# Gate and up projections of 18 feed-forward tiles as seven block products over 2x2x2 blocks

## The chip, the cores and the metric

The kernel runs on one core of a Trainium2 chip. The metric is the device time of one execution in microseconds (us). The core has five engines that run side by side: TensorE (PE) multiplies matrices, VectorE (DVE) and ScalarE (ACT) work element by element, GpSimd (POOL) and SyncE (SP) issue DMAs. Each takes its instructions in the order in which the program issued them. PEld in the profile is TensorE's loading of weights, which overlaps its matmuls.

## The reference

Two layers of a backbone over 512 latent tokens and 256 context tokens, 1024 wide: a modulated RMS norm, attention beside a long convolution, a gated merge, an output projection, and then a feed-forward part. The part that the change touches is the feed-forward:

```python
def swiglu(h, w_gate_up, w_down):
    g, u = jnp.split(h @ w_gate_up, 2, axis=-1)
    return (jax.nn.silu(g) * u) @ w_down

for layer in range(DEPTH):          # DEPTH = 2
    ...
    if not last:
        ctx = ctx + c_gate2 * swiglu(modulate(rms_norm(ctx, ...), c_shift2, c_scale2), ...)
    x = x + gate2 * swiglu(modulate(rms_norm(x, ...), shift2, scale2), ...)
```

The inner width is 2816, that is 22 tiles of 128. Layer one (index 0) runs it over all 768 tokens, layer two over the 512 latent ones.

## The kernel before

Everything is kept transposed: a tile holds 128 channels in the partitions and the tokens along the free axis. Each float32 operand is split into a high part and a low part of a shorter format (`fp32r`), and a product is the sum of three matmuls, high by high, high by low and low by high (`mm3`, L237). For weights the split is one ACT copy (`act`, L248) and one DVE subtraction (`tt`, L258). Weights come by DMA into one of five `raw` buffers; `w_load` (L333) splits each into a `hi` and a `lo` buffer (four of each, 1024 columns wide), and `w_more` (L353) starts the next load when a `raw` is free, in the order of a list, `plan` (L311).

The order of the work is made while the kernel is built. Each piece of work is a Python generator that yields what it needs: tiles, free buffers, events. `Order.go` (L159) keeps an estimate of each engine's time from fixed costs. Among the tasks that are ready by TensorE's time it takes the one of lowest priority number, else the one that is ready first, and so writes one fixed instruction order for each engine. Buffers are counted too: 37 of `s` (768 wide), 13 of `f` (1024 wide), eight PSUM banks `ps`; `t` is a short-lived `s`.

The feed-forward of a layer (L1385) goes by groups of tiles, `GROUPS`, six, six, six and four. For each tile `job` (L548) streams all eight k blocks of the gate weights, first over tokens 0 to 512, then 512 to 768, 24 matmuls each; then the same for up. The first two tiles of a layer use `pair_job` (L575), gate and up side by side. `g_evac` makes tanh on ACT and a product on DVE (`stt`, L254); `u_evac` multiplies by up and splits the result into a pair `pr`, which goes into `mids`. When a group's tiles are through, the down projection multiplies its `mids` for eight output tiles, and `resid` (L1216) adds each to the stream `xs` on DVE. The first two output tiles run as a `pair_job`, k block by k block, so that the last of `mids` is needed last. The last group runs through `parts` (L595) over the token ranges `END` (0 to 256, 256 to 512, 512 to 768), so that the next layer's norm can begin.

Beside this runs `mod_rest` (L444): the rest of the modulation vectors, 80 tiles of 128 channels, each a 512 KB DMA into a `raw` buffer and one or two multiply-and-reduce instructions on DVE (L458). It is spawned once in layer one at `j == START` (L1306) and again ahead of the merge (L1360), with priority 0; tiles from `CALM` on, and those of layer two, wait until the norms before the feed-forward are done.

## Time and profile before

| what | value |
|---|---|
| median of 3 runs | 2166.92 us (2166.75 to 2167.97) |
| the profiled execution: its time | 2169.32 us |
| its span, first to last instruction | 2167.5 us |
| mean granted TensorE clock | 0.994 of full speed |
| moved by DMA | 256.72 MB, mean 118 GB/s |
| longest stretch of the last chain on TensorE alone | 521.48 us from 753.29 us, in layer one's feed-forward |

The span runs from the first to the last instruction; the device time also has what lies around it. A stage's rows give busy time by engine. In a group of instructions, "busy" is the sum over the group, "mean ns" the duration of one, and "idle before" the time its engine stood still just ahead of them, with what ended most of it. Matmuls overlap, so what one costs is read from the distance between their starts.

### The profile page before, as it was taken

What the parts mean: (1) busy time and instruction counts of PE and PEld (TensorE: products, weight loads), DVE (VectorE), ACT (ScalarE), POOL (GpSimd) and SP (SyncE); (2) the same over time, 40 slices, a digit from 0 to 9 for tenths busy, and PEclk for the clock granted to TensorE, in tenths of its full rate; (3) what the DMA queues carried; (4) which work ended last, traced back from release to release, by engine and by line L of the source; (5) the groups of instructions that cost most, each with busy time, mean ns of one, the idle gap of its engine ahead of it and who ended that gap; (6) DMA issues with size and microseconds to landing.
All of it is one profiled execution on the core that took longest, in us unless ns stands there. A gap on an engine that the chain in (4) does not pass through costs nothing.

```text
span 2167.5 us, 30309 instructions
## 1 busy us (share of the span) xinstructions
PE 2129.8 (98%) x12001; PEld 1837.0 (85%) x12001; DVE 1388.0 (64%) x2550; ACT 732.1 (34%) x1336; POOL 117.1 (5%) x218
## 2 busy tenths in 40 slices
PE   8999999999999999999999999999999999999997
PEld 2889888888888888888888897887888898888887
DVE  5878637767896798743333468756877665434354
ACT  3433223445522421131221334223545343222231
POOL 2112100001000000000000010200001000000000
PEclk9999999999999999999999999999999999999999
DMA  9234422113375267832212332532213433323231
GB/s 361 74 125 160 144 73 73 40 60 126 108 232 186 79 200 227 266 99 73 66 52 78 107 109 85 190 100 89 73 54 117 154 133 96 109 81 110 80 110 39
DMA packets 83053, 256.72 MB, mean 118 GB/s; under 512 B 10668, under 2 KB 15183, under 8 KB 82912
## 3 DMA queue, kind: packets, MB, share of 16 engines
q1 hardware_dynamic: 63840, 197.43, 27.9%
q0 software_dynamic: 19072, 57.36, 8.2%
q8 instruction: 94, 1.54, 0.3%
q14 instruction: 47, 0.39, 0.1%
HBM read 232.07 MB, written 22.68 MB: 118 GB/s over the span
## 4 chain that ended last, share of the span: by engine, by line
PE 88%; DVE 7%; issue 3%; ACT 1%; DMA 1%; POOL 0%; SPq 0%; DVEq 0%; ACTq 0%; POOLq 0%
PE ps L234 85%; PE ps L244 3%; DVE f L258 2%; DVE s L254 2%; DVE s L258 1%; DVE lo L258 1%; ACT s L248 1%; DVE mx L269 0%; DMA s<-in_rcos 0%; DVE ss L269 0%; DVE s L263 0%; DVE rq L258 0%; DMA f<-in_wmodf 0%; ACT hi L248 0%; DVE rq L254 0%
## 5 line engine op out<-in xcount | busy, mean ns | idle before, releaser
L234 PE MATMUL ps<-s,hi 128*128 128x512 f32 (+1 forms) x4288 | 1132.5, 353 | 8.9 <-ACT s L248 5.9
L234 PEld LDWEIGHTS ps<-s,hi 128*128 128x128 f32 x4288 | 749.1, 190 | 117.8 <-ACT s L248 8.7
L234 PE MATMUL ps<-s,lo 128*128 128x512 f32 (+1 forms) x2144 | 751.0, 350 | 0.1
L234 PEld LDWEIGHTS ps<-s,lo 128*128 128x128 f32 x2144 | 406.4, 190 | 54.3 <-DVE lo L258 0.6
L248 ACT ACTIVATE hi<-raw 128x1024 fp32r<-128x1024 f32 (+2 forms) x272 | 268.6, 995 | 469.0 <-PE ps L234 329.9
L258 DVE TENSOR_TENSOR lo<-raw,hi 128x1024 fp32r<-128x1024 f32 (+2 forms) x272 | 309.1, 1142 | 100.0 <-ACT hi L248 97.6
L234 PE MATMUL ps<-f,hi 128*128 128x512 f32 (+1 forms) x1184 | 297.0, 341 | 0.0
L254 DVE SCALAR_TENSOR_TENSOR s<-s,ps 128x512 f32<-128x512 f32 (+1 forms) x184 | 107.0, 586 | 267.6 <-ACT s L248 143.7
L234 PEld LDWEIGHTS ps<-f,hi 128*128 128x128 f32 x1184 | 205.0, 190 | 25.3
L248 ACT ACTIVATE s<-ps 128x256 f32<-128x256 f32 (+5 forms) x234 | 107.7, 482 | 314.9 <-PE ps L234 236.4
L234 PE MATMUL ps<-f,lo 128*128 128x512 f32 (+1 forms) x592 | 201.5, 340 | 0.0
L254 DVE SCALAR_TENSOR_TENSOR s<-ps,mod,s 128x256 f32<-128x256 f32 (+1 forms) x144 | 82.9, 585 | 152.0 <-PE ps L234 151.7
L234 PE MATMUL ps<-hi,s 128*128 128x512 f32 x512 | 165.2, 395 | 0.0
L234 PE MATMUL ps<-f 128*128 128x256 f32 (+1 forms) x1014 | 141.9, 289 | 4.0 <-DMA f<-in_fw 3.8
L248 ACT ACTIVATE f<-ps 128x512 fp32r<-128x512 f32 (+3 forms) x184 | 91.3, 538 | 137.4 <-PE ps L234 85.5
L234 PEld LDWEIGHTS ps<-f 128*128 128x128 f32 (+1 forms) x1014 | 129.5, 191 | 7.3 <-DMA f<-in_z 3.8
L234 PEld LDWEIGHTS ps<-f,lo 128*128 128x128 f32 x592 | 112.2, 189 | 12.6
L248 ACT ACTIVATE s<-ps,nb 128x256 f32<-128x256 f32 (+1 forms) x144 | 80.7, 568 | 109.0 <-DVE nb L263 105.0
L234 PEld LDWEIGHTS ps<-hi,s 128*128 128x128 f32 x512 | 97.0, 189 | 19.5
L458 DVE CUSTOM_DVE_ANT_0 raw<-raw,f 128x1024 f32<-128x1024 f32 x80 | 97.9, 1224 | 23.7 <-DMA raw<-in_wmodt 21.9
L269 DVE TENSOR_REDUCE mx<-ps 128x1 f32<-128x512 f32 (+1 forms) x104 | 68.4, 684 | 61.0 <-PE ps L234 61.0
L258 DVE TENSOR_TENSOR f<-ps,f 128x512 fp32r<-128x512 f32 (+2 forms) x144 | 90.7, 654 | 24.9 <-ACT f L248 24.1
(118 smaller groups left out, 1803.8 us busy)
## 6 DMA issues: line engine op xcount, KB each, us to landing
raw<-in_w_gu SPq DMA_DIRECT2D x88, 512.0 KB, 3.7
raw<-in_wmodt SPq DMA_DIRECT2D x80, 512.0 KB, 4.3
raw<-in_w_down SPq DMA_DIRECT2D x48, 384.0 KB, 3.2
raw<-in_w_gate SPq DMA_DIRECT2D x32, 512.0 KB, 3.7
raw<-in_w_hy SPq DMA_DIRECT2D x24, 512.0 KB, 4.6
raw<-in_w_qkv SPq DMA_DIRECT2D x24, 512.0 KB, 3.7
raw<-in_w_out SPq DMA_DIRECT2D x24, 512.0 KB, 3.9
f<-in_tab POOLq DMA_DIRECT2D x40, 256.0 KB, 5.2
```

Source lines behind the costliest of these rows:

```text
L234: nc.tensor.matmul(out=o, lhsT=l, rhs=r, start=start, stop=stop)
L244: nc.tensor.transpose(o, x, ident[0:n, 0:n])
L248: nc.scalar.activation(out=o, in_=i, func=f, **kw)
L254: nc.vector.scalar_tensor_tensor(out=o, in0=a, scalar=s, in1=b, op0=op0, op1=op1)
L258: nc.vector.tensor_tensor(out=o, in0=a, in1=b, op=op)
L269: nc.vector.tensor_reduce(out=o, in_=a, op=op, axis=AX.X)
L458: nc.vector.tensor_tensor_reduce(out=junk[:, 0:D], in0=raw, in1=cond[s], scale=1.0, scalar=0.0, op0=ALU.mult, op1=ALU.add, accum_out=mraw[ ...
```

## The change

Gate and up of tiles 4 to 21 in layer one are computed together. With the weights cut into two halves of k (four blocks of 128 each) by gate and up, and the activations into the two halves of k by two halves of the tokens (384 each), the result is a 2x2 block product. It is made from seven block products in place of eight (Strassen's scheme in Winograd's form). Each product streams 4 k blocks x 3 matmuls of 384 columns.

- `s_load` gets the two raw weight tiles of a feed-forward tile, makes four sums of weight halves on DVE and splits the seven forms, each 512 columns, into halves of the `hi` and `lo` buffers.
- `s_forms` makes four forms of the activations once, for all 18 tiles. From the second k block on, and for the form T3, which is written over part of the activations themselves, it waits until the first group's plain products are issued (`plain`).
- `s_job` issues the seven products; `sums` adds them up on DVE into gate and up (`g`, `c`), `silu` and `times` do by halves of the tokens what `g_evac` and `u_evac` did.
- Groups in layer one: 4, 4, 4, 2, 4 and 4 tiles; the first of these is computed as before. Layer two keeps its groups.
- `w_load` takes its buffers in the order of the list (`turn`), and the last group's down weights wait for `room`.
- `mod_rest` runs at priority 0 or 3 and fetches one tile ahead. `START` 5 is beyond the loop over j, so only the second call does work. Some priorities, the number of attention lanes, the order of gate jobs and how far loads run ahead have other values.

```diff
-GROUPS = ((0, 6), (6, 6), (12, 6), (18, 4))
+GROUPS = (((0, 4), (4, 4), (8, 4), (12, 2), (14, 4), (18, 4)), ((0, 6), (6, 6), (12, 6), (18, 4)))
+PLAIN = (4, 22)
+LATE = 1
+MODP = (0, 3)
+FORMP = (0, 0, 1)
+HALF = TOK // 2
...
-LANES, MORE_LANES = (2, 10), (4, 5)
+LANES, MORE_LANES = (2, 9), (1, 4)
-CALM = 40
+CALM = 43
-START = 3
+START = 5
-FIRST_W, AHEAD = 4, 2
-CONV, SPEC, TURN, ROPE, LANE, HYP, NORM2, LONG, STORE, SPLIT = -3, 3, 4, -1, 4, -10, 4, 3, 4, -5
+FIRST_W, AHEAD = 4, 3
+CONV, SPEC, TURN, ROPE, LANE, HYP, NORM2, LONG, STORE, SPLIT = -3, -2, 4, -5, 4, -12, 2, 3, 3, -5
-MIX = ((4, 2, 2, 1), (3, 2, 2, 1))
+MIX = ((4, 2, 2, 1), (4, 2, 4, 1))
...
     def w_load(i, src, nk, nf, one=False):
...
-        yield [raw_n] + ([("f", 1)] if one else [("hi", 1), ("lo", 1)])
-        if one:
+        room = Cond(lambda: len(od.free["f"]) > 3 or gu_done[0].set and (od.free["f"] or len(od.free["s"]) > 20))
+        yield [raw_n, turn[i]] + ([room] if one else [("hi", 1), ("lo", 1)])
+        if one and not od.free["f"]:
+            tiles = [new("t", F32R) for _ in range(2)]
+            hi, lo = tiles[0][:, 0:n], tiles[1][:, 0:n]
+        elif one:
...
+    def s_load(i, src):
+        g, u = new("raw"), new("raw")
+        for x, y in zip((g, u), (src[0], src[1])):
+            dma(x.rearrange("p (k f) -> p k f", k=KD), y, nc.sync)
+        halves = lambda x: (x[:, 0:512], x[:, 512:1024])
+        (g0, g1), (u0, u1) = halves(g), halves(u)
...
+        steps = ((g0, ()), (g0, ((u0, u0, u1, ALU.add), (g0, u0, g0, ALU.subtract))), (g1, ()),
+                 (g0, ((g1, g1, g0, ALU.subtract), (g0, u1, g0, ALU.subtract))), (u0, ()), (g1, ()), (u1, ()))
+        for e, (x, ops) in zip(res, steps):
+            for o, y, z, op in ops:
+                yield [y, z]
+                tt(o, y, z, op)
+            f = yield from forms.place()
...
+            hi, lo = [y.rearrange("p k f -> p (k f)") for y in f[0]]
+            yield [x]
+            act(hi, x)
+            yield [hi]
+            tt(lo, x, hi, ALU.subtract)
...
+    def prod(form, b):
+
+        yield [form, ("ps", 1)]
+        o = new("ps")[:, 0:HALF]
+        (wh, wl), tiles, left = form.form
+        for k in range(4):
+            yield [b[k][2]]
+            yield [wh[:, k, :], wl[:, k, :], b[k][0], b[k][1]]
+            mm3(o, wh[:, k, :], wl[:, k, :], b[k][0], b[k][1], k == 0, k == 3)
+        forms.done(tiles, left)
+        return o
+
+    def s_job(B, pr, got):
...
+        def times(sl, o):
+            yield [cut[sl is b], got]
+            yield [o]
+            stt(t[:, sl], t[:, sl], 0.5, o, ALU.mult, ALU.mult)
+            yield [t[:, sl]]
+            act(pr[0][:, sl], t[:, sl])
+            yield [pr[0][:, sl]]
+            tt(pr[1][:, sl], t[:, sl], pr[0][:, sl], ALU.subtract)
...
+        def sums():
...
+            act(g[:, a], P[0])
...
+            tt(g[:, b], g[:, a], P[1], ALU.add)
...
+            tt(g[:, a], g[:, a], P[2], ALU.add)
...
+            tt(c[:, a], g[:, b], P[3], ALU.add)
...
+            tt(g[:, b], g[:, b], P[4], ALU.add)
+            tt(c[:, b], c[:, a], P[4], ALU.add)
...
+            tt(g[:, b], g[:, b], P[5], ALU.add)
...
+            tt(c[:, a], c[:, a], P[6], ALU.add)
...
+        for n, (x, y) in enumerate(((A11, B11), (S2, T2), (A12, B21), (S3, T3), (S1, T1), (S4, B22), (A22, T4))):
+            P[n] = yield from prod(x, y)
+            made[n].set = True
+
+    def s_forms(h, B, plain):
...
+            if k == LATE:
+                yield [plain]
...
+            tt(a, ah, al, ALU.add)
+            tt(b, bh, bl, ALU.add)
+            tt(a[:, a_], a[:, b_], a[:, a_], ALU.subtract)
+            tt(a[:, b_], b[:, b_], a[:, b_], ALU.subtract)
+            tt(b[:, b_], b[:, b_], a[:, a_], ALU.subtract)
+            tt(b[:, a_], b[:, a_], b[:, b_], ALU.subtract)
...
-                    od.spawn(mod_rest(stop, [stop]), 0)
+                    od.spawn(mod_rest(stop, [stop]), MODP[0])
...
-                od.spawn(mod_rest(Event(), calm), 0)
+                od.spawn(mod_rest(Event(), calm), MODP[1])
...
-            for gi, (f0, fn) in enumerate(GROUPS):
+            plain = Event()
+            if not last:
...
+                od.spawn(s_forms(h, B, plain), FORMP[0])
+            for gi, (f0, fn) in enumerate(GROUPS[l]):
                 mids = []
                 for f in range(f0, f0 + fn):
...
+                    if f >= PLAIN[l]:
+                        pr, got = [], Event()
+                        if f < FFT - 1:
+                            yield [("f", 2)]
+                            pr += [new("f", F32R) for _ in range(2)]
+                            got.set = True
+                        yield from s_job(B[0:7], pr, got)
+                        mids.append(pr)
+                        if f == FFT - 1:
+                            drop(*[x for p in h for x in p], *B[7])
+                            yield [("s", 2)]
+                            pr += [new("s", F32R) for _ in range(2)]
+                            got.set = gu_done[l].set = True
+                        continue
```

More of the change, by code (lines that the diff above doesn't have):

```diff
@@ L344, in w_load @@
             hi, lo = tiles[0][:, 0:n], tiles[1][:, 0:n]
-        loaded[i] = [x.rearrange("p (k f) -> p k f", k=nk) for x in (hi, lo)] + [tiles]
+        turn[i + 1].set = True
+        loaded[i] = [x.rearrange("p (k f) -> p k f", k=nk) for x in (hi, lo)] + [tiles, one]
         w_here[i].set = True
@@ L351, in w_load, with __init__, place, done @@
         w_more()
+    class Forms:
+        def __init__(self):
+            self.half = None
+        def place(self):
+            if self.half:
+                tiles, left = self.half
+                self.half = None
+                c = 512
+            else:
+                yield [("hi", 1), ("lo", 1)]
+                tiles, left = [new("hi", F32R), new("lo", F32R)], [2]
+                self.half = tiles, left
+                c = 0
+            return [x[:, c:c + 512].rearrange("p (k f) -> p k f", k=4) for x in tiles], tiles, left
+        def done(self, tiles, left):
+            left[0] -= 1
+            if not left[0]:
+                drop(*tiles)
+                at[2] -= 1
+                w_more()
@@ new lines, in hyena_body @@
+    forms = Forms()
+    def s_load(i, src):
[4 more added lines that the diff above has]
+        (g0, g1), (u0, u1) = halves(g), halves(u)
+        res = loaded[i] = [Event() for _ in range(7)]
+        for e in res:
+            e.form = None
+        w_here[i].set = True
+        yield [g, turn[i]]
+        steps = ((g0, ()), (g0, ((u0, u0, u1, ALU.add), (g0, u0, g0, ALU.subtract))), (g1, ()),
[5 more added lines that the diff above has]
+            f = yield from forms.place()
+            e.form, e.set = f, True
+            if e is res[-1]:
+                turn[i + 1].set = True
+            hi, lo = [y.rearrange("p k f -> p (k f)") for y in f[0]]
[3 more added lines that the diff above has]
+            tt(lo, x, hi, ALU.subtract)
+        drop(g, u)
+        w_more()
@@ L353, in w_more @@
     def w_more(upto=INF):
         while at[1] < min(len(plan), upto) and od.free["raw"]:
-            one = len(plan[at[1]]) > 3
-            if not od.free["f"] if one else at[2] >= SLOTS["hi"] + AHEAD:
+            e = plan[at[1]]
+            if len(e) == 1:
+                if len(od.free["raw"]) < 2:
+                    break
+                at[1] += 1
+                at[2] += 4 - at[3] % 2
+                at[3] += 1
+                od.spawn(s_load(at[1] - 1, *e), FORMP[2])
+                continue
@@ L357, in w_more @@
+            one = len(e) > 3
+            if not (od.free["f"] or len(od.free["s"]) > 8) if one else at[2] >= SLOTS["hi"] + AHEAD:
                 break
@@ L446, in mod_rest, with fetch @@
         yield from load_cond(cond)
-        while rest and not stop.set:
-            yield [("raw", 1)]
-            if rest[0][1] >= CALM or rest[0][0]:
-                yield calm
-                yield [("raw", 1)]
+        ahead = []
+        early = lambda: rest[0][1] < CALM and not rest[0][0] or all(e.set for e in calm)
+        def fetch():
             l, t, both = rest.pop(0)
@@ L454, in mod_rest @@
             dma(raw, I["wmodt"][l, t], nc.sync)
+            ahead.append((l, t, both, raw))
+        while ahead or rest and not stop.set:
+            if not ahead:
+                yield [("raw", 1)]
+                if not early():
+                    yield calm
+                    yield [("raw", 1)]
+                fetch()
+            if rest and not stop.set and len(od.free["raw"]) > 1 and early():
+                fetch()
+            l, t, both, raw = ahead.pop(0)
             yield [raw, ("t", 1), "DVE"] + cond
@@ new lines, in s_forms, with third @@
+    def s_forms(h, B, plain):
+        a_, b_ = slice(0, HALF), slice(HALF, TOK)
+        B11, B21, B22, T1, T2, T3, T4 = B[0:7]
+        for k in range(4):
+            (ah, al), (bh, bl) = h[k], h[k + 4]
+            if k == LATE:
+                yield [plain]
+            yield [ah, al, bh, bl, ("f", 2), ("t", 4 if k % 2 == 0 else 2)]
+            a, b = new("f"), new("f")
+            a, b = a[:, 0:TOK], b[:, 0:TOK]
+            tA = [new("t", F32R) for _ in range(2)]
+            if k % 2 == 0:
+                tB = [new("t", F32R) for _ in range(2)]
+                B[7].extend(tB)
+            B[7].extend(tA)
+            tt(a, ah, al, ALU.add)
[4 more added lines that the diff above has]
+            tt(b[:, a_], b[:, a_], b[:, b_], ALU.subtract)
+            h2 = b_ if k % 2 else a_
+            for form, x, sl in ((T1, tA, a_), (T2, tA, b_), (T4, tB, h2)):
+                form[k][0:2] = [y[:, sl] for y in x]
+                form[k][2].set = True
+            for x, (hi, lo, _) in ((b[:, b_], T2[k]), (a[:, a_], T1[k]), (b[:, a_], T4[k])):
+                yield [x]
+                act(hi, x)
+                yield [hi]
+                tt(lo, x, hi, ALU.subtract)
+            drop(b)
+            def third(a=a, k=k):
+                yield [plain]
+                act(T3[k][0], a[:, b_])
+                yield [T3[k][0]]
+                tt(T3[k][1], a[:, b_], T3[k][0], ALU.subtract)
+                drop(a)
+                T3[k][2].set = True
+            od.spawn(third(), FORMP[1])
@@ L1426, in program @@
                     mids.append(pr)
+                    plain.set = f == PLAIN[l] - 1
                 yield [x[:, 40:48] for x in m[0:2 - last]]
-                if gi == len(GROUPS) - 1:
-                    drop(*[x for p in h for x in p])
+                if gi == len(GROUPS[l]) - 1:
+                    if last:
+                        drop(*[x for p in h for x in p])
                     end = stag if last else END
```

87 lines of the change are left out of this document (76 added, 11 removed).

## The prediction

> **What bounds the kernel now.** I read the page first: who is busy, and the chain that ended last.
>
> ```profile
> span 2167.5 us, 30309 instructions
> PE 2129.8 (98%) x12001; PEld 1837.0 (85%) x12001; DVE 1388.0 (64%) x2550; ACT 732.1 (34%) x1336; POOL 117.1 (5%) x218
> PE 88%; DVE 7%; issue 3%; ACT 1%; DMA 1%; POOL 0%; SPq 0%; DVEq 0%; ACTq 0%; POOLq 0%
> ```
>
> TensorE is busy for 98% of the span, and 88% of the last chain is its own instructions. A busy PE need not be an efficient one, so the next question is where it is ever idle. The windows view answers by stage (columns: window, its length, then busy us with the number of instructions of PE, PEld, DVE, ACT, POOL, then clock, DMA share, GB/s):
>
> ```profile
> 0.00:55.00 55.00, 45.56 (x125) 13.27 (x126) 32.26 (x70) 21.27 (x36) 11.71 (x26) 0.94 0.99 356
> 520.00:604.00 84.00, 81.83 (x545) 73.04 (x544) 75.96 (x169) 43.47 (x111) 6.79 (x12) 1.00 0.42 141
> 604.00:690.00 86.00, 86.00 (x479) 75.32 (x478) 77.21 (x120) 21.19 (x25) 2.15 (x4) 1.00 0.67 223
> 690.00:753.00 63.00, 62.56 (x380) 55.33 (x379) 40.93 (x83) 23.21 (x37) 0.00 (x0) 1.00 0.25 83
> 753.00:1275.00 522.00, 521.99 (x3058) 464.14 (x3057) 284.44 (x463) 116.55 (x178) 0.00 (x0) 1.00 0.39 123
> 1275.00:1310.00 35.00, 30.34 (x203) 26.71 (x203) 31.97 (x96) 18.12 (x42) 10.76 (x20) 0.99 0.46 144
> 1475.00:1700.00 225.00, 220.74 (x1266) 192.01 (x1266) 170.90 (x356) 114.12 (x263) 17.17 (x32) 1.00 0.29 93
> ```
>
> The feed-forward of layer one fills 753 to 1275 us (its first tiles begin a little before). PE is idle there for 0.01 us of 522, at full clock: this stage costs exactly the columns that it streams. DVE has 284 of 522 busy, ACT 117. So fewer streamed columns shorten it one for one, as long as nobody else becomes late.
>
> **What the products save.** What a matmul costs is its spacing, not its duration, which overlaps the next. The timeline of PE alone (start, us, operation) shows one gate or up job, eight k blocks of three matmuls, first over 512 tokens, then over 256:
>
> ```profile
> 823.78 0.63 PE L234 MATMUL ps<-s,hi 128*128 128x512 f32 x2
> 829.25 0.40 PE L234 MATMUL ps<-s,hi 128*128 128x256 f32 x2
> 832.12 0.63 PE L234 MATMUL ps<-s,hi 128*128 128x512 f32 x2
> 840.46 0.63 PE L234 MATMUL ps<-f,hi 128*128 128x512 f32 x2
> ```
>
> 24 matmuls of 512 take 829.25 - 823.78 = 5.47 us, 0.228 each; 24 of 256 take 2.87, 0.1196 each. Gate and up of one tile: 840.46 - 823.78 = 16.68 us. No row has 384 columns; the bounds are 0.1196 (a 256) and 0.228 (a 512). I take the middle, 0.1738, since the two points give a line of 0.42 ns a column with 11 ns on top, and loading weights keeps pace even with 256-column matmuls. A new tile is seven products of 4 x 3 matmuls of 384: 84 x 0.1738 = 14.60 us, **2.08 less**, and 18 tiles give **37.4 us**. At the ends of the bound a tile is 10.0 or 19.2, the second slower than now; a cost that jumps between 256 and 512 is excluded by nothing but the line, and it goes to the slow rival. The Trainium skill, "TensorE: Matmul & The Clock Gate", section Back-to-back issue gap, gives N/2.4 + 2.5 ns for an isolated matmul; by it a tile would go from 15.6 to 13.65 us and the saving would be an estimated 35 us. The trace's 0.228 and 0.1196 lie 10 ns above the page's 0.216 and 0.109, so the rows decide.
>
> The down projection keeps its columns: six groups instead of four split the same 22 tiles.
>
> **What it adds on DVE and ACT.** The groups by line in the same stage (count | busy us, mean ns | idle before):
>
> ```profile
> L458 DVE CUSTOM_DVE_ANT_0 raw<-raw,f 128x1024 f32<-128x1024 f32 x56 | 68.5, 1223 | 22.9 <-DMA raw<-in_wmodt 21.9
> L258 DVE TENSOR_TENSOR lo<-raw,hi 128x1024 fp32r<-128x1024 f32 x44 | 53.7, 1222 | 14.7 <-ACT hi L248 14.7
> L254 DVE SCALAR_TENSOR_TENSOR s<-s,ps 128x512 f32<-128x512 f32 x44 | 30.1, 685 | 83.5 <-ACT s L248 46.2 <-PE ps L234 37.1
> L458 DVE CUSTOM_DVE_ANT_0 s<-raw,f 128x1024 bf16<-128x1024 f32 x24 | 29.2, 1217 | 0.4 <-DMA raw<-in_wmodt 0.4
> L258 DVE TENSOR_TENSOR lo<-raw,hi 128x768 fp32r<-128x768 f32 x24 | 22.7, 955 | 4.0 <-ACT hi L248 4.0
> L254 DVE SCALAR_TENSOR_TENSOR s<-s,ps 128x256 f32<-128x256 f32 x44 | 18.4, 418 | 34.9 <-ACT s L248 23.8 <-PE ps L234 10.8
> L254 DVE SCALAR_TENSOR_TENSOR s<-ps,mod,s 128x512 f32<-128x512 f32 x24 | 17.8, 749 | 35.4 <-PE ps L234 35.4
> L254 DVE SCALAR_TENSOR_TENSOR s<-ps,mod,s 128x256 f32<-128x256 f32 x35 | 16.4, 481 | 27.9 <-PE ps L234 27.9
> L258 DVE TENSOR_TENSOR f<-s,f 128x512 fp32r<-128x512 f32 x17 | 11.7, 690 | 8.4 <-ACT f L248 8.4
> L258 DVE TENSOR_TENSOR f<-s,f 128x256 fp32r<-128x256 f32 x17 | 7.1, 417 | 0.0
> L458 DVE DVE_READ_ACCUMULATOR2_ANT mraw<- 128x1 f32 x80 | 6.5, 82 | 0.0
> L258 DVE TENSOR_TENSOR f<-raw,f 128x512 fp32r<-128x512 f32 x8 | 5.3, 686 | 1.3 <-ACT f L248 1.3
> L248 ACT ACTIVATE f<-s 128x512 fp32r<-128x512 f32 x17 | 10.8, 633 | 96.2 <-DVE s L254 96.2
> L248 ACT ACTIVATE f<-s 128x256 fp32r<-128x256 f32 x17 | 6.9, 408 | 8.2 <-DVE s L254 7.9
> ```
>
> A tile now costs DVE 2 x 1.222 (weights) + 2 x (0.685 + 0.418) (tanh product, times up) + 0.690 + 0.417 (low part) = 5.76 us. After: weights, 4 sums and 7 low parts of 512, 11 x 0.686; evacuation, 7 sums, 2 + 2 products and 2 low parts of 384, 13 x 0.553 (midway between 0.417 and 0.690, the ends of the bound). 7.55 + 7.19 = **14.74 us**, against 14.60 on PE. That looks like a tie, but these durations overlap a little: the twelve DVE rows above add up to 287, without the smaller groups, where the window has 284 busy. I allow up to 8% off: 13.6 to 14.7.
>
> DVE recovers in the down pass. Four tiles of down are 8 x 4 x 3 matmuls of each size, 96 x (0.228 + 0.1196) = 33.4 us of PE, and on DVE 8 x (0.686 + 0.749 + 0.481) = 15.3. So a group of four has 4 x 14.60 + 33.4 = 91.8 us on PE and 4 x 14.74 + 15.3 = 74.3 on DVE, 81%. Forms can be split ahead into eight half buffers (four hi and lo pairs), more than one tile's seven, so DVE has about a tile's slack inside a group. ACT: 7 splits at 0.633 and 5 pieces at about 0.52 (midway of 0.408 and 0.633), 7.0 us a tile: never the bound.
>
> Once per layer: the activation forms, per k block 2 x 0.955 + 8 x 0.553, four times 25.3 us, written while the plain first group (4 x 16.68 + 33.4 = 100 us of PE) runs. The two extra groups add 16 x (0.749 + 0.481) = 19.7 us. In all DVE gains 18 x 9.0 + 25.3 + 19.7 = about 207 us on top of 284, in a stage of 485: **near full**. What decides is whether full DVE means late PE. These stretches of before say no:
>
> ```profile
> 756.00:790.00 34.00, 34.00 (x200) 30.18 (x199) 33.24 (x56) 9.45 (x15) 0.00 (x0) 1.00 0.56 184
> 790.00:835.00 45.00, 45.00 (x258) 39.71 (x258) 44.13 (x76) 11.15 (x18) 0.00 (x0) 1.00 0.65 203
> 1000.00:1100.00 100.00, 100.00 (x585) 88.77 (x584) 34.97 (x48) 20.67 (x29) 0.00 (x0) 1.00 0.22 70
> ```
>
> From 756 to 835 DVE has 77.4 of 79 busy, and PE loses nothing; later DVE is at 35%. The filler is the modulation reduction (the two custom groups, 97.7 us). After, it runs at priority 3, below the form and evacuation tasks at 0, so it yields: with 36 us free in the plain group (100 - 4 x 5.76 - 15.3 - 25.3) and 17 to 25 in each later one, it ends between 1030 and 1190 us instead of 925, and only the next layer wants it.
>
> **What it adds as waits.** Down cannot start before the last tile's `mids` are there. Each hop has a price: a job's last matmul of three starts at 707.62, the next job 0.23 later, and DVE answers at 708.05.
>
> ```profile
> 707.62 0.39 PE L234 MATMUL ps<-s,lo 128*128 128x512 f32 x1
> 708.05 0.75 DVE L254 SCALAR_TENSOR_TENSOR s<-ps,mod,s 128x512 f32<-128x512 f32 x1 [3.30 <-PE ps L234]
> ```
>
> After the seventh product: 0.20 + three DVE steps of 0.553 + one ACT step of 0.52 = 2.4 us alone; the other half's chain (begun one product, 2.09 us, earlier) and one or two weight splits of 0.686 stand in the same queue: 3.2 to 3.9. The cover is the down job's first blocks: 3 x 6 x 0.228 = 4.1 us with four tiles, so nothing to 1 us more when a reduction of 1.22 cuts in (three ends, I take 0.5 each); 6 x 0.228 = 1.37 in the group of two: 2.0; 18 x 0.1196 = 2.15 before the last block in the last group, which starts on 256 tokens: 1.5. Sum **5.0 us** (bounds 0 and 19: at worst each of five ends waits 3.9 less the smallest cover, plus a reduction). Behind these waits only the down matmuls are queued. In the last group at most one down weight is split ahead; the second costs 0.633 + 0.686 = 1.3 us in the shadow of the same chain.
>
> **What moves elsewhere.** Four early reduction tiles (from 204 to 251 us) go away from there, with two broadcasts on POOL's queue, and `CALM` 43 lets three more run early.
>
> ```profile
> L277 SPq DMA_DIRECT2D raw<-in_wmodt x80: 327/328/1554, 182.5 to 919.3; - x80
> L458 DVE CUSTOM_DVE_ANT_0 s<-raw,f x4: 1215/1215/1217, 203.8 to 249.6; 128x1024 bf16<-128x1024 f32 x4
> L458 DVE CUSTOM_DVE_ANT_0 raw<-raw,f x16: 1224/1224/1228, 604.2 to 668.9; 128x1024 f32<-128x1024 f32 x16
> raw<-in_w_gu SPq DMA_DIRECT2D x88, 512.0 KB, 3.7
> ```
>
> So 7 x 2.44 = 17 us more of DVE between 540 and the norm near 716; before, the last ends at 670, so it ends near 690, in the 690 to 753 stage with 22 us free. On SP's queue there are 16 more issues of 0.33 us, hidden like its others; a new tile's two raw blocks land 3.7 us after issue, two of the five raw buffers hold a pair, and the next pair has 14.6 us to come. Other lanes, gate order and priorities: the stages around hold 2.2 + 0.4 + 4.7 + 4.3 = 11.6 us of PE idle in the windows above that they could win or about double. I take 0, bounds -8 and +10.
>
> **Sum.** -37.4 + 5.0 + 0 = -32.4. The profiled execution took 2169.3 us (span 2167.5 and 1.8 around it); it goes to 2136.9. It lay 2.4 above the median 2166.9, so the median goes to **2134.5 us**.
>
> **Rivals.**
> - *DVE partly late.* If each tile runs at DVE's 14.74 plus 0.7 of waits that its queue can't fill, 0.84 x 18 = 15 us are lost: 2150. For: 81% in a group, full with the reductions. Against: 756 to 835. It includes ends that stall over 3.4 us; there the Trainium skill (same page, section on the clock gate) has a rule that an idle window of about 3.4 us halves the clock. In this trace the 0 to 55 stage with 9.4 us idle had 0.94, the one at 1275 with 4.7 us in pieces 0.99, so it adds little. 0.17.
> - *DVE in strict order behind ACT: slower.* Each of the nine low parts needs the ACT result just before it, and two products need a tanh. If the queue can't fill these eleven waits, DVE needs 14.74 + 7 x 0.633 + 4 x 0.52 = 21.3 us a tile. Break-even is 16.68, with 1.94 of those 6.5 exposed; at half (18.0) the tiles lose 61 us and the kernel goes to 2195. The Trainium skill, "VectorE: DVE Perf Modes", section on the TRN2 errata, speaks against small pieces too: a fixed cost per instruction, so at least 512 elements. The rows agree (1.222 at 1024, 0.417 at 256: 0.15 us fixed), and it is in the sum. Against the rival: 14.7 us idle behind ACT in 44 low parts now. With matmuls of 384 costing over 0.1986 (16.68/84), the other way to lose, 0.06.
> - *The retuning wins as well*: 8 us of the idle elsewhere, 2126. 0.12.
> - *No gain reaches the end*: the layer boundary after 1275 waits for the late reductions or DMAs instead. It would need 32 us; the reductions have 50 us of margin, and the first sixteen, which the next norm reads, far more. 0.03.
>
> **Chances.** The forecast has 0.62 (2128 to 2144). A measurement tells 0.2%, 4 us, from no change. Faster: 0.62 + 0.12 + 0.16 of the partly late case = 0.90; same 0.04 (0.01 of that case and the last); slower 0.06. The range takes in the retuning's gain and most of the partly late case: 2120 to 2156, with 0.83 inside.
>
> **What would show it.** Right: in the feed-forward of layer one 1512 matmuls of 384 columns spaced 0.174 us, a stage shorter by 30 to 37 us, DVE 85% or more busy, reductions on beyond 1000 us. Wrong: PE waits for `hi` or `lo` inside a tile (DVE is the bound), waits over 2 us at the ends of groups of four, spacing over 0.18, or stages outside that differ by over 10 us.

## The result and the profile after

The changed kernel takes **2153.02 us**, the median of four runs (2148.8 to 2155.55), against 2167.14 for the kernel before beside it (2166.75 to 2167.97): a ratio of **0.9932, 95% interval 0.9915 to 0.9950**. It is 14 us faster where 32 were forecast. (Of the kernels below, two had one run far longer than the rest at a lower granted clock, as had the kernel before; medians and ratios leave these out.) The profiled execution took 2152.17 us, 17.15 less than that of before.

The first lines of the page after:

```profile
span 2150.4 us, 30465 instructions
PE 2100.6 (98%) x11785; PEld 1839.0 (86%) x11785; DVE 1567.1 (73%) x2926; ACT 786.8 (37%) x1476; POOL 115.1 (5%) x216
PE 69%; DVE 18%; issue 5%; DMA 5%; ACT 1%; SPq 0%; POOL 0%; DVEq 0%; ACTq 0%; POOLq 0%
```

TensorE's busy time fell by 29.2 us (2129.8 to 2100.6), the span by only 17.1. And the last chain has changed hands: DVE holds 18% of it instead of 7, DMA 5 instead of 1. TensorE's timeline inside the products (start, us, operation):

```profile
862.07 0.51 PE L246 MATMUL ps<-s,hi 128*128 128x384 f32 x2
...
881.83 0.51 PE L246 MATMUL ps<-s,hi 128*128 128x384 f32 x2
```

From 862.07 to 881.83 lie 38 sets of three, 114 matmuls in 19.76 us: 0.1733 each, without a gap. The saving is there. The windows view of after shows where it went (busy us of PE, PEld, DVE, ACT, POOL; then clock, DMA share, GB/s):

```profile
690.00:750.00 60.00, 56.88 (x334) 51.01 (x332) 52.60 (x93) 21.41 (x32) 0.00 (x0) 0.94 0.45 142
750.00:800.00 50.00, 49.69 (x285) 43.43 (x285) 44.23 (x89) 16.11 (x29) 0.00 (x0) 1.00 0.37 113
800.00:900.00 100.00, 97.60 (x557) 91.62 (x557) 94.95 (x172) 34.49 (x67) 0.00 (x0) 0.98 0.30 95
900.00:1000.00 100.00, 97.66 (x553) 92.80 (x552) 93.18 (x168) 32.14 (x60) 0.00 (x0) 0.98 0.42 133
1000.00:1100.00 100.00, 96.13 (x548) 88.84 (x547) 88.19 (x161) 28.51 (x54) 0.00 (x0) 1.00 0.48 157
1100.00:1200.00 100.00, 99.75 (x573) 95.18 (x573) 89.42 (x161) 35.20 (x65) 0.00 (x0) 1.00 0.41 130
1200.00:1262.00 62.00, 59.41 (x391) 58.97 (x390) 51.66 (x103) 27.34 (x51) 0.00 (x0) 1.00 0.34 107
1262.00:1300.00 38.00, 36.13 (x223) 31.09 (x223) 32.78 (x99) 18.63 (x42) 10.75 (x20) 1.00 0.45 132
```

A stage loses PE's idle time, plus its length times what the clock falls short of 1. The feed-forward lost 0.01 us before (753 to 1275); now its six rows, 750 to 1262, have 11.8 us idle, and two have clock 0.98, 2 us each: about 16. The stage ahead of it (690 to 750) has 3.1 idle and clock 0.94, 6.7 together, against 0.4 before. DVE has 462 of 512 us busy in the feed-forward, up to 95% in a stretch.

To close the account over the whole trace, I added up how far each matmul stands from the next beyond the usual distance of its shape (0.227, 0.173 and 0.120 us for 512, 384 and 256 columns). That loss was 56.4 us before and is 77.4 after. With the feed-forward taken from 744 to 1275 us before and from 750 to 1262 after, it went there from 2.5 to 20.7; in the stretch from 604 us up to it from 0.5 to 6.6; everywhere else from 53.4 to 50.1, with gains and losses. Saved columns: 18 x (48 x (0.227 + 0.120) - 84 x 0.173) = 38.2 us. 38.2 less 21.0 is 17.2, the 17.1 of the spans.

The two largest waits of TensorE between 760 and 1262 us (us in total, times, longest):

```profile
PE ps L246 <- ACT f L260: 5.7, 4, 2.3
PE ps L246 <- DVE f L270: 3.0, 3, 2.0
```

What DVE did around the stall at 912 us, and then TensorE, by the timeline:

```profile
908.73 1.23 DVE L556 CUSTOM_DVE_ANT_0 s<-raw,f 128x1024 bf16<-128x1024 f32 x1
...
910.00 1.23 DVE L556 CUSTOM_DVE_ANT_0 raw<-raw,f 128x1024 f32<-128x1024 f32 x1
...
911.15 1.01 DVE L270 TENSOR_TENSOR f<-f,ps 128x384 f32<-128x384 f32 x2
912.08 0.68 DVE L270 TENSOR_TENSOR lo<-raw,hi 128x512 fp32r<-128x512 f32 x1
912.68 1.61 DVE L266 SCALAR_TENSOR_TENSOR f<-f 128x384 f32<-128x384 f32 x3
```

```profile
908.17 0.33 PE L246 MATMUL ps<-s,lo 128*128 128x384 f32 x1
...
912.24 0.39 PE L246 MATMUL ps<-f,lo 128*128 128x512 f32 x1
914.91 1.39 PE L246 MATMUL ps<-f,hi 128*128 128x512 f32 x2 [2.28 <-ACT f L260]
```

The group's last product ends near 908.4. Its last sums start on DVE only at 911.15, behind a pair of reductions that began at 908.73. PE covers 4 us with the first blocks of down and then stands still for 2.28 us. No line names the reduction as the culprit: the waits view names the last hop, ACT. One has to read DVE's queue backwards from there. The other large stalls up to here: 3.0 us at 714.8 (the out-projection's sum behind reductions up to 713.84), 2.0 at 820.4, 1.5 at 1008.3, 1.75 at 1070.2 and 2.0 at 1241.5. All of PE's waits in the feed-forward from 760 us on stand at ends of groups, none inside a tile.

### The profile page after: what moved, and what is told of

Its sections match the earlier page's. It is cut to its first block, busy times and chain, and to the rows that moved or that the text cites. A ratio compares the mean times of both kernels' runs of the same rounds, so it can differ in the third digit from the quotient of the medians.

```text
span 2150.4 us, 30465 instructions
## 1 busy us (share of the span) xinstructions
PE 2100.6 (98%) x11785; PEld 1839.0 (86%) x11785; DVE 1567.1 (73%) x2926; ACT 786.8 (37%) x1476; POOL 115.1 (5%) x216
## 4 chain that ended last, share of the span: by engine, by line
PE 69%; DVE 18%; issue 5%; DMA 5%; ACT 1%; SPq 0%; POOL 0%; DVEq 0%; ACTq 0%; POOLq 0%
PE ps L246 67%; DVE lo L270 3%; DVE f L270 3%; DMA raw<-in_wmodt 3%; PE ps L256 2%; DVE s L266 2%; DVE raw L556 2%; DVE s L556 2%; DMA f<-in_wmodf 1%; DVE f L266 1%; DVE s L270 1%; DVE raw L270 1%; ACT s L260 1%; DVE mx L281 1%; DMA f<-in_tab 0%
## 5 line engine op out<-in xcount | busy, mean ns | idle before, releaser
L246 PE MATMUL ps<-s,hi 128*128 128x512 f32 (+2 forms) x4112 | 1097.4, 352 | 7.0 <-ACT s L260 3.1
L246 PEld LDWEIGHTS ps<-s,hi 128*128 128x128 f32 x4112 | 728.3, 189 | 91.4 <-ACT s L260 5.4
L246 PE MATMUL ps<-s,lo 128*128 128x512 f32 (+2 forms) x2056 | 719.9, 350 | 0.1
L260 ACT ACTIVATE hi<-raw 128x512 fp32r<-128x512 f32 (+3 forms) x378 | 307.3, 832 | 491.5 <-PE ps L246 301.6
L270 DVE TENSOR_TENSOR lo<-raw,hi 128x512 fp32r<-128x512 f32 (+3 forms) x378 | 350.5, 941 | 90.6 <-ACT hi L260 86.7
L260 ACT ACTIVATE s<-ps 128x512 f32<-128x512 f32 (+5 forms) x190 | 86.5, 480 | 212.6 <-PE ps L246 134.9
L266 DVE SCALAR_TENSOR_TENSOR s<-s,ps 128x512 f32<-128x512 f32 (+1 forms) x96 | 58.9, 618 | 142.6 <-ACT s L260 72.4
L260 ACT ACTIVATE f<-ps 128x512 fp32r<-128x512 f32 (+4 forms) x210 | 103.8, 533 | 155.6 <-PE ps L246 108.8
L246 PEld LDWEIGHTS ps<-f 128*128 128x128 f32 (+1 forms) x1122 | 145.1, 192 | 11.8 <-DMA f<-in_z 3.8
L260 ACT ACTIVATE f<-f 128x384 f32<-128x384 f32 (+5 forms) x110 | 72.5, 665 | 188.9 <-DVE f L270 134.9
L270 DVE TENSOR_TENSOR f<-f 128x512 f32<-128x512 f32 (+6 forms) x152 | 117.7, 798 | 7.1 <-ACT f L260 5.2
```

What stands on the lines that cost most here:

```text
L246: nc.tensor.matmul(out=o, lhsT=l, rhs=r, start=start, stop=stop)
L260: nc.scalar.activation(out=o, in_=i, func=f, **kw)
L266: nc.vector.scalar_tensor_tensor(out=o, in0=a, scalar=s, in1=b, op0=op0, op1=op1)
L270: nc.vector.tensor_tensor(out=o, in0=a, in1=b, op=op)
```

## The experiments

The theory after the result: **DVE's queue is nearly full and keeps its written order, and long work that can wait (reductions, activation forms, weight splits) stands in it ahead of the short chains that TensorE needs.** Rivals: the retuned constants lose what the products save; the products' own chain at a group's end is too long whatever stands in the queue; loads that land late at the head of the queue. Ratios are to the kernel before beside them, with their 95% intervals; its medians there lay between 2167 and 2172 us.

**The changed kernel once more** (no edit):

> The changed kernel as it is, beside the others on the same chip. A ratio of 0.992 to 0.995 to before, as at first; the stalls at 714, 820, 912, 1008, 1070 and 1241 us are in its fixed order and come again, the halved clock behind them only where a stall fills one of the clock's windows, so single runs differ by a few us.

2153.29 us, 0.9915 (0.9899 to 0.9930). The stalls are at the same places. Half clock followed those at 714, 820 and 912 us, and in this run those at 1008 and 1241 too.

**The layer-two reductions left out:**

```diff
+                if l:
+                    nc.vector.memset(mraw[s][:, t:t + 1], 1.0)
+                    ...
+                    continue
```

> The changed kernel, with the modulation reductions of layer two left out on DVE (a one-column memset stands for each; their loads stay), so its output is not the reference's. Theory Q: the stalls at the ends of the groups come from what stands in DVE's queue ahead of the last tile's chain, reductions first; the ends at 912, 1008 and 1070 us lose their 1.6 to 2.4 us each and the halved clock after them goes too: about 9 us faster than the changed kernel, 2144. Rival S: the chain behind the seventh product is longer than its cover, reductions or not: the ends stay, 2152 or more.

2137.28 us, 0.9854 (0.9836 to 0.9873). Windows of this kernel, then of the changed one:

```profile
800.00:1200.00 400.00, 398.68 (x2295) 379.50 (x2294) 316.66 (x614) 138.15 (x256) 0.00 (x0) 1.00 0.39 124
```

```profile
800.00:1200.00 400.00, 391.14 (x2226) 368.45 (x2226) 365.74 (x659) 130.34 (x245) 0.00 (x0) 0.99 0.40 129
```

With DVE at 317 instead of 366, the stalls at 820, 912 and 1008 are gone. The chain at a group's end was not too long by itself: with nothing ahead of it, four tiles of down cover it, as forecast. What stays are the group of two (1.2 us) and the last group (2.0 us), about the 2.0 and 1.5 forecast. By the matmuls' distances the same feed-forward matmuls lose 9.5 us here and 20.7 in the changed kernel, so the layer-two reductions account for some 11 of the 18 us that were lost anew. The time comes within 3 us of the forecast.

**Two halves of the change.** Everything but the products (groups of six, no product tile), and the products with the old constants:

```diff
-PLAIN = (4, 22)
+PLAIN = (22, 22)
...
```

> The changed kernel without the seven products: all 22 tiles and groups of six as before, and every other edit kept (lanes, priorities, gate order, CALM, START, prefetch). Theory R: the stop of 3.2 us at 714 us and the slow clock behind it (6.2 us together) come from these edits, and 180 to 300 us and the layer boundary win about 7: within 4 us of before, 2163 to 2171. Rival: the products themselves bring the stop at 714 us, then these edits alone are a gain of 5 us or more, 2162 or less.

```diff
-CALM = 43
+CALM = 40
-START = 5
+START = 3
(and LANES, MORE_LANES, AHEAD, the priorities, MIX as before the change)
```

> The changed kernel with the constants of before (lanes, CALM 40, START 3, priorities, gate order, AHEAD 2); products, groups and form tasks as changed. Theory R: the stop at 714 us goes, since four reduction tiles run early again and three more wait, and the gain at 180 to 300 us is lost: 2150 to 2153, no better. Rival: the retuning is what costs, then it lies at 2146 or less.

2176.19 us, 1.0028 (1.0017 to 1.0040), and 2170.1 us, 0.9994 (0.9984 to 1.0004). Neither half gains; together they do. The products with old constants had been expected at 2150 to 2153 us. The constants alone bring the stall near 712 us (4.7 us, and half clock behind it), so it doesn't come from the products. The products with old constants lose their gain in layer two; PE's timeline and a window of that kernel:

```profile
1415.96 0.79 PE L246 MATMUL ps<-f 128*128 128x256 f32 x2 [6.98 <-ACT f L260]
```

```profile
1300.00:1475.00 175.00, 165.77 (x860) 141.60 (x859) 120.45 (x189) 57.67 (x88) 23.16 (x43) 0.96 0.39 124
```

Here 9.2 us idle and 7 us of clock are lost, where the changed kernel loses 2.6 and 1.75 in the same window. The convolution's chain through DVE and ACT has nothing beside it on PE. So the retuning is no gain on top of the products; it keeps layer two's work beside that chain.

**Which constants.** The old priorities alone, and the old lanes and gate order alone:

```diff
-CONV, SPEC, TURN, ROPE, LANE, HYP, NORM2, LONG, STORE, SPLIT = -3, -2, 4, -5, 4, -12, 2, 3, 3, -5
+CONV, SPEC, TURN, ROPE, LANE, HYP, NORM2, LONG, STORE, SPLIT = -3, 3, 4, -1, 4, -10, 4, 3, 4, -5
```

> The changed kernel with the task priorities of before (SPEC 3, ROPE -1, HYP -10, NORM2 4, STORE 4). Theory P: the filter spectrum of layer two comes as late again as before, its convolution's long DVE chain stands alone at 1408 us, and 8 to 12 us of the gain go. Rival: within 3 us of the changed kernel.

```diff
-LANES, MORE_LANES = (2, 9), (1, 4)
+LANES, MORE_LANES = (2, 10), (4, 5)
-MIX = ((4, 2, 2, 1), (4, 2, 4, 1))
+MIX = ((4, 2, 2, 1), (3, 2, 2, 1))
```

> The changed kernel with the attention lanes and the order of gate jobs of before. Theory P: these matter little: within 4 us of the changed kernel. Rival: the order of gate jobs in layer two is what fills the wait at 1408 us: 8 to 12 us slower.

2160.82 us, 0.9956 (0.9941 to 0.9972), and 2162.45 us, 0.9955 (0.9939 to 0.9970). Each is worth 7 to 9 us; without it the stall near 1405 us stands there as with all the old constants, with 3.85 and 6.6 us. That the lanes and the gate order matter so much was not expected.

**The reductions kept out of a group's last tile** until down has begun:

```diff
-            yield [raw, ("t", 1), "DVE"] + cond
+            yield [raw, ("t", 1), "DVE", quiet] + cond
...
+                    quiet.set = f < f0 + fn - 1
```

> The changed kernel with one gate more: a reduction may not be put into the queue from the start of a group's last tile until the first two output tiles of its down projection are issued. Same work. Theory Q: the ends at 912, 1008 and 1070 us shrink to under 1 us each, with the clock at full speed behind them; 820 us (activation forms) and 1241 us (a heap of down weights to split) stay: 2145 to 2148. Rival S: the same stalls, 2152 or more.

2151.58 us, 0.9910 (0.9897 to 0.9923): no gain that can be told from the changed kernel. But look at its windows:

```profile
800.00:1200.00 400.00, 398.69 (x2293) 379.25 (x2293) 356.35 (x640) 135.32 (x256) 0.00 (x0) 1.00 0.33 104
1262.00:1300.00 38.00, 31.05 (x137) 23.70 (x136) 32.54 (x77) 19.08 (x36) 4.29 (x8) 0.91 0.33 92
```

From 800 to 1200 us the feed-forward runs as well as with the reductions left out, though all of them are still done. The ends of the groups of four cost next to nothing as soon as no reduction stands ahead; that is the clearest proof of the mechanism. (The group of two keeps 1.2 us and the last group 2.0, as above.) The reductions then run on past the feed-forward, to 1473 us, and the boundary to layer two loses 7.0 us idle and 3.4 of clock, against 1.9 in the changed kernel. 1300 to 1475 loses 2 us more. What was won is paid back there.

**Shorter and combined gates.** Gated from the fifth product of the last tile, forms behind the plain group's work (`FORMP` 2, 2, 1), the last group's down weights behind its sums:

> The changed kernel with three edits of order: reductions kept out of the queue from the fifth product of a group's last tile until the down pair is issued (a shorter gate than the first one), activation forms at priority 2, the last group's down weights at priority 1. Theory Q: stalls at 820, 912 and 1008 us under 0.7 us, at 1241 under 1.5; reductions still end before the layer does: 6 to 10 us faster than the changed kernel on the same chip. Rival: the reductions pile up at the layer's end as under the longer gate and take it back: within 2 us.

2160.73 us, 0.9948 (0.9930 to 0.9965): 7 us slower than the changed kernel beside it. From 1200 to 1300 us it loses 11.7 us idle and has clock 0.95.

**Forms later, alone** (`FORMP` 2, 2, 1):

> The changed kernel with the activation forms' tasks at priority 2 in place of 0, so that the last plain tile's evacuation goes first. Theory Q: the stall at 820 us (2.2 us, with 3.4 us of half clock behind) goes, the rest stays; TensorE's order is the same. Rival S: it stays, since the chain itself is too long.

2155.0 us, a single run. The stall at 820 us is gone. In the changed kernel forms stand right ahead of the plain group's last low part:

```profile
817.69 1.82 DVE L270 TENSOR_TENSOR f<-s 128x768 f32<-128x768 f32 x2
...
822.28 0.42 DVE L270 TENSOR_TENSOR f<-f 128x256 fp32r<-128x256 f32 x1
```

But with the reductions left out or held back, and the forms at their old priority, the stall is gone too: there the forms are written behind this low part (815.35 and 816.15 us in the gated kernel). So forms and reductions make it together. With the forms late, a stall of 1.6 us comes at 852 instead, and the one at 909 grows to 4.3.

**Seven reduction tiles fewer ahead of the norm** (`CALM` 40, `START` 3, as before the change: four tiles run at 200 to 250 us again, three only in the feed-forward):

> The changed kernel with CALM 40 and START 3 again: four modulation tiles run at 200 to 250 us and three wait until after the norm, so seven fewer are in the queue before 714 us. Theory R: the stall there (3.2 us with 3.4 of slow clock behind it) goes, some 2 to 4 us come back at 180 to 300 us and three tiles more crowd the feed-forward: 2 to 4 us faster than the changed kernel. Rival: the stall is not these seven but DVE's waiting for loads of reduction tiles that arrive late: no change.

2153.61 us, 0.9921 (0.9907 to 0.9936). Windows:

```profile
690.00:750.00 60.00, 59.70 (x362) 52.76 (x360) 38.20 (x76) 21.72 (x34) 0.00 (x0) 1.00 0.34 112
900.00:1000.00 100.00, 93.86 (x523) 88.84 (x522) 93.04 (x168) 30.90 (x57) 0.00 (x0) 0.95 0.42 133
```

The stall ahead of the feed-forward is gone (DVE 38 instead of 53): 6.4 us. The stretch from 900 loses 11.1 instead of 4.3: two pairs of reductions, at 902.05 and 906.46, stand ahead of the same group's end. 6.4 won, 6.8 given back.

**The last 32 reductions of layer two behind its attention**, then also with `CALM` 40 and `START` 3, the forms later and the last group's down weights behind its sums:

> The changed kernel with the reductions of layer two for its last 32 modulation tiles (40 us of DVE) moved behind the attention of layer two, as those of layer one are, where DVE is half idle. Nothing is left out. Theory D: the stalls at 912 and 1008 us and some of the slow clock go: 5 to 9 us faster than the changed kernel. Rival: they cost as much at their new place, where the norm before the second feed-forward waits for them: no change.

> As the one before, and with CALM 40 and START 3, the activation forms at priority 2 and the last group's down weights at priority 1. Theory D: with room on DVE the stops at 714, 820 and 1241 us can go without coming back elsewhere: 12 to 17 us faster than the changed kernel, near 2138. Rival: they come back as before, and it is no better than the deferral alone.

2165.16 us, 0.9985 (0.9974 to 0.9996), and 2166.55 us, 0.9988 (0.9977 to 0.9998). With the first, the feed-forward gets better (1.3 us idle from 1000 to 1200, against 4.1), but 1475 to 1700 now has 6.8 idle against 2.95, and 1700 to 1784 has 4.7 against 2.0. Layer two isn't emptier where it counts. The second is no better: the stall ahead of 913 us grows to 6.1.

**The other sign: 64 additions of 1024 columns more on DVE**, beside the layer-two reductions:

```diff
+                if l and not both:
+                    for _ in range(2):
+                        nc.vector.tensor_tensor(out=cond[1], in0=cond[0], in1=cond[0], op=ALU.add)
```

> The changed kernel with 64 additions of 1024 columns more on DVE, two behind each reduction of the last 32 tiles of layer two, results unused: about 73 us more for DVE in or after the feed-forward of layer one. Theory D: DVE has no 73 us to spare there, so the stalls grow and reductions run into the layer's end: 10 to 25 us slower than the changed kernel. Rival Q alone (only what happens to stand ahead of a group's end matters): within 5 us.

2193.72 us, 1.0111 (1.0094 to 1.0128). 71 us more of DVE (1637.8 busy against 1566.9) cost 40 us of time, more than either side had expected:

```profile
800.00:1200.00 400.00, 372.57 (x2079) 349.45 (x2078) 383.19 (x647) 121.50 (x228) 0.00 (x0) 0.96 0.34 109
```

At 96% DVE, PE has 27 us idle in this stretch, where it had 9. Here DVE is the bound.

**Part of DVE's work given to GpSimd**, the 72 sums of weight halves:

```diff
-                tt(o, y, z, op)
+                nc.gpsimd.tensor_tensor(out=o, in0=y, in1=z, op=op)
```

> The changed kernel with the four weight sums of each new tile on GpSimd in place of VectorE: 72 x 0.69 = 50 us less of DVE work in the feed-forward, GpSimd otherwise idle there. Theory D (DVE's work between 750 and 1170 us is as much as it can do, so a stall removed at one place comes back at another, and only less work for DVE helps): 5 to 10 us faster than the changed kernel, 2143 to 2148. Rival: the sums come late from GpSimd, or slow DVE down beside it, and TensorE waits for weight forms instead: 2153 or slower.

2192.65 us, 1.0110 (1.0093 to 1.0126). Groups of that kernel and, below, of the changed one, 750 to 1262 us (count | busy, mean ns | idle before):

```profile
L418 POOL TENSOR_TENSOR raw<-raw 128x512 f32<-128x512 f32 x72 | 102.8, 1436 | 526.4 <-DMA raw<-in_w_gu 311.8 <-issue 109.3 <-DVE lo L270 75.9
L270 DVE TENSOR_TENSOR lo<-raw,hi 128x512 fp32r<-128x512 f32 x155 | 109.6, 728 | 55.8 <-ACT hi L260 55.1
L270 DVE TENSOR_TENSOR f<-f 128x384 fp32r<-128x384 f32 x32 | 21.7, 689 | 1.4 <-ACT f L260 1.2
```

```profile
L270 DVE TENSOR_TENSOR raw<-raw 128x512 f32<-128x512 f32 x72 | 49.6, 689 | 1.4
L270 DVE TENSOR_TENSOR lo<-raw,hi 128x512 fp32r<-128x512 f32 x158 | 104.8, 686 | 3.1 <-ACT hi L260 1.6
L270 DVE TENSOR_TENSOR f<-f 128x384 fp32r<-128x384 f32 x34 | 18.3, 554 | 2.2 <-ACT f L260 1.8
```

GpSimd needs 1.44 us for a sum that takes DVE 0.69. The weight forms become the late ones (DVE stands 55 us behind their high parts). And some of DVE's instructions grow, which the means hide: of the 155 low parts of weights, the 14 that ran while a GpSimd sum ran took 1.16 us on average, the other 141 took 0.684. Of the 32 low parts of 384, the ten beside a GpSimd sum took 0.99 on average, the other 22 took 0.553. Sums with one operand in PSUM (`f<-f,ps`) did not grow: 0.546 us for the 20 beside a GpSimd sum, 0.547 for the others.

**Fewer product tiles** (first eight plain), and that with `CALM` 40, `START` 3 and the down weights behind the sums:

```diff
-PLAIN = (4, 22)
+PLAIN = (8, 22)
```

> The changed kernel with the first eight tiles plain in place of four, so 14 tiles by seven products. It gives up 4 x 2.1 = 8.5 us of matmuls. Theory D: with 9 us less of DVE work a tile in the second group, the reductions end some 100 us earlier, the stalls at 820, 912 and 1008 us (6.5 us, with slow clock 10) mostly go: within 3 us of the changed kernel. Rival: stalls are the same wherever new tiles are: 8 us slower.

> As the one before, with CALM 40 and START 3, so that the stop at 714 us goes (5 us with its slow clock), and with the last group's down weights at priority 1. Theory D: DVE has room now for the three tiles that move into the feed-forward: 4 to 7 us faster than the one before. Rival: as with four plain tiles the gain is given back: no faster.

2161.64 us, 0.9954 (0.9942 to 0.9966), and 2157.08 us, 0.9943 (0.9928 to 0.9958). The first is 8.4 us slower than the changed kernel, just the columns of four tiles (4 x 2.1). From 800 to 1200 us the loss did not shrink (16.7 us by the matmuls' distances, against 15.8), although DVE has less to do, and that speaks against fill alone. The timeline of DVE shows one reason:

```profile
914.47 0.68 DVE L266 SCALAR_TENSOR_TENSOR f<-f,ps 128x512 f32<-128x512 f32 x1
917.67 1.23 DVE L556 CUSTOM_DVE_ANT_0 raw<-raw,f 128x1024 f32<-128x1024 f32 x1 [2.52 <-DMA raw<-in_wmodt]
```

DVE stands idle for 2.52 us at a reduction whose load hasn't landed; the chain's next step, a low part of 512, follows it at 918.82.

**Late loads taken out**: the planner counts on a modulation load 4.5 us after its issue instead of 2, alone and with three edits (`CALM` 40 and `START` 3, forms later, down weights behind the sums):

```diff
-            dma(raw, I["wmodt"][l, t], nc.sync)
+            dma(raw, I["wmodt"][l, t], nc.sync, 4.5)
```

> One number of the planner is changed: it takes a modulation load to land 4.5 us after issue instead of 2, so that a reduction is put into DVE's order later, behind more of the short chains, and its load has landed when DVE comes to it. The work is the same. Theory 'a late load at the head of DVE's queue makes the stalls': DVE's idle time behind the modulation loads (15.3 us in 9 places in the changed kernel) goes, the group ends lose about half of their stalls, 2142 to 2147 us. Theory 'DVE's order and its fill make them': the idle time behind the loads goes, but the reductions themselves still stand ahead of the chains; the stalls move and the time stays within 2150 to 2157 us.

> The later landing of the modulation loads in the plan together with three more reductions early (START 3, CALM 40, as before the change), activation forms at priority 2 ahead of the plain group's work, and the last group's down weights behind its sums at priority 1. Theory 'late loads at the head of the queue': 2136 to 2144 us, as the out-projection stall, the 820 us stall and the ends of groups go together. Theory 'order and fill': the stall near 714 us and the one near 820 us go, and 4 to 8 us of stalls come back later in the feed-forward or at the layer boundary; 2148 to 2158 us.

2172.53 us, 1.0011 (1.0002 to 1.0021), and 2157.82 us, 0.9941 (0.9921 to 0.9960). DVE's idle time ahead of reductions, in the changed kernel and in the first of these:

```profile
  DMA raw<-in_wmodt: 18.4, 13
```

```profile
  DMA raw<-in_wmodt: 3.5, 4
```

The late loads are nearly gone, and the kernel is 19 us slower, beyond what either theory expected. The reductions now come later as a whole, up to 1418 us instead of 1179, and those that the feed-forward's norm reads are the last ones before it; DVE's timeline:

```profile
743.18 1.22 DVE L556 CUSTOM_DVE_ANT_0 s<-raw,f 128x1024 bf16<-128x1024 f32 x1
...
745.71 0.24 DVE L270 TENSOR_TENSOR mod<-mraw,bmod 128x8 f32<-128x8 f32 x2
```

```profile
690.00:770.00 80.00, 61.86 (x353) 53.79 (x352) 71.38 (x140) 27.08 (x44) 0.00 (x0) 0.87 0.39 127
800.00:900.00 100.00, 100.00 (x582) 93.22 (x581) 90.19 (x161) 32.61 (x64) 0.00 (x0) 1.00 0.32 101
```

The second fence is of the same kernel's windows: 18 us idle ahead of the feed-forward, then a stretch from 800 without any loss. But the next group's end, at 926, stands for 3.9 and 1.5 us behind a pair of reductions at 919.61 that waited for no load. By the matmuls' distances the whole feed-forward loses 19.9 us, against 20.7 in the changed kernel. With the three edits the loss ahead of the feed-forward is small again (2.6 us from 690 to 750), and 1262 to 1300 us loses 12 us. So late loads are not what makes the stalls at the groups' ends; which chain meets the reductions is what counts.

At 714 us this is less clear. The changed kernel's DVE stood 5.5 us for loads ahead of reductions between 683 and 702. With the layer-two reductions left out, the reductions up to 716 us are the same 54, DVE stood there for 3.1 us, and PE has 0.8 us idle from 690 to 750 instead of 3.1; but PE had already stood for 1.84 us at 602 there. Seven tiles fewer take this stall away, so the reductions are needed for it; how much of it the late loads add stays open.

## Why the prediction was wrong

What held, step by step:
- *What the products save*: 0.173 us for 384 columns against the 0.1738 taken; 38.2 us against 37.4. By the gap that the Trainium skill gives ("TensorE: Matmul & The Clock Gate", section Back-to-back issue gap) it would have been an estimated 35; the rows were the better guide.
- *What it adds on DVE and ACT*: 0.686, 0.549 to 0.555 and 0.52 us, as taken; DVE near full (90% of the feed-forward), the reductions to 1180 us.
- *Inside a tile* PE doesn't wait: the strict-order rival is out. The layer boundary was no trap either: 1.9 us idle in 1262 to 1300, where before had 4.7 in 1275 to 1310.
- *The group of two and the last group*, taken as 2.0 and 1.5, have 2.3 and 2.6 us idle at their ends (1.2 and 2.0 in the largest stalls without the layer-two reductions): the chains were priced about right.

**The step that failed is "What it adds as waits": 5.0 us, where the feed-forward lost 18 more than before.** Its bounds, 0 and 19, held that; the value taken in them didn't. The premise was that a reduction at priority 3 "yields", so that one of 1.22 us would cut in now and then for 0.5 us. The priority acts while the order is written: it ranks the tasks that are ready at that point. A sum that still waits for its product isn't ready, a reduction is, and so it goes into the queue first, as a pair of 2.44 us. On the chip nothing yields: for the stall at 912 us the pair starts at 908.73, just as the product ends, and the sums wait behind it until 911.15. The same holds for the first group, which I put at 0: forms and reductions cost 2.0 us there, and half clock behind it. In the sum the reductions had 1.5 us, 0.5 at each of three ends; leaving those of layer two out takes some 11 us off the feed-forward's loss. Waits over 2 us at the ends of groups of four were the prediction's own sign of being wrong, and 820 and 912 show it.

The trace of before had shown it, right behind the stretch that I took as evidence. From 756 to 835, with a full DVE, no group ends; the first end comes at 840.46. DVE of before, just there (timeline):

```profile
840.08 1.22 DVE L458 CUSTOM_DVE_ANT_0 s<-raw,f 128x1024 bf16<-128x1024 f32 x1
...
842.76 0.68 DVE L254 SCALAR_TENSOR_TENSOR s<-s,ps 128x512 f32<-128x512 f32 x1
843.36 1.22 DVE L458 CUSTOM_DVE_ANT_0 raw<-raw,f 128x1024 f32<-128x1024 f32 x1
...
845.44 1.22 DVE L458 CUSTOM_DVE_ANT_0 raw<-raw,f 128x1024 f32<-128x1024 f32 x1
```

Four reductions stand in that chain too. PE doesn't see them, since six tiles give down five finished ones to begin with: 30 matmuls, 6.8 us. Groups of four leave three, 4.1 us, and the chain of sums is longer.

Two smaller terms. *"What moves elsewhere"* was taken as 0: 690 to 750 loses 6 us, because the 22 us counted as free there lie between the steps of the out-projection's chain, and the reductions, some of them waiting for their loads, stand among them. Elsewhere 3 us were won. And *the clock* "adds little": of the loss, about 7 us are half clock (three stretches of 6.83, 3.41 and 3.41 us at 0.5 behind the stalls at 714, 820 and 912), not idle time.

In sum: 38.2 instead of 37.4, 18 instead of 5, 3 instead of 0 elsewhere; 17.2 instead of 32.4 by the spans. The two medians differ by 3 us less, as the profiled run of before lay 2.2 above its median and the one of after 0.85 below. The rival "DVE partly late" (2150 us) named the right time and engine, but charged it to tiles; the tiles are free and the group ends pay. That its time, and with it the slow part of the range, came so near is luck.

What stays open: whether another order of the same work would win the 13 to 17 us that leaving the layer-two reductions out is worth (by the ratios, 0.9854 against 0.9915 and 0.9932), and how much late loads add at 714 us. Most of the moves tried took stalls away at one place and gave them back at another, and none beat the changed kernel clearly. That shows that these don't do it, not that none does.

## What to carry to other kernels

When work moves from a full engine to one that becomes nearly full, price each short chain that the full engine waits for by what can stand in front of it in the other's queue: the longest deferrable piece, whole, and in pairs where it is written in pairs. A priority in a planner orders what is ready; it doesn't interrupt, and free time counted in a window is of no use if it lies between the steps of a chain. Test it by leaving the deferrable work out and by moving it: if the first wins and the second doesn't, its cost is its place, and the next place must be priced before it is moved.

## What the runs showed of the hardware

- Stalls of 2 to 3 us were followed by half clock in some places and not in others. In the changed kernel 3.02 us idle ahead of 718.08 was followed by 6.83 us at 0.5, and 2.04 us ahead of 822.75 and 2.28 us ahead of 914.91 by 3.41 each; there a 512-column matmul came every 0.43 us instead of 0.227. Stalls of 1.75 and 1.99 us at 1070 and 1241 had none behind them. In the second profile of the same kernel, the stalls at 1008 and 1241, 1.75 and 1.99 us long, did have 3.41 us of it behind them, so the length of the stall alone does not decide; what does is not shown. The Trainium skill, "TensorE: Matmul & The Clock Gate", section on the HAM clock gate, puts the drop after at least one idle window of about 3.4 us; here shorter ones sufficed, in some places and not in others. That a stall costs its clock as well was the dearer half at 714 us: 3.1 idle, 3.6 clock.
- A GpSimd sum of 128x512 took 1.44 us against DVE's 0.69. DVE's own sums and splits of two operands in SBUF took longer only while such a sum ran: on average 1.16 instead of 0.684 us for 512 columns, and 0.99 instead of 0.553 for the low part of 384. Those with an operand in PSUM took the same, 0.546 and 0.547.
